# Follow-up work of the input projection in two queues instead of one, with scratch tiles of its own for gMLP

## The chip, the cores and the metric

One core of a Trainium2 chip runs one layer of a hybrid model in float32. The metric is the device time of the kernel in microseconds (us). The kernel before takes 3417.4 us, the median of 3 runs (3416.64 to 3420.89). The engines are named as in the profile: PE is TensorE (PEld its weight loads), DVE is VectorE, ACT is ScalarE, POOL is GpSimd, SP is SyncE.

## What is computed

640 tokens (512 latent ones on a grid, 128 of context) of width 2048 go through one layer:

- RMSNorm and modulation give h. `p = h @ w_in` has 5440 columns: r, k and v of 1024 columns each for 16 heads, low-rank inputs of 64, 64 and 160 columns, and u and v of 1024 each for 8 gMLP groups.
- The heads (RWKV-7): after a token shift, decays and gates are made from the low-rank inputs, and a delta-rule scan runs over the tokens in both directions:

```python
def step(S, inp):
    r_t, w_t, k_t, v_t, a_t, b_t = inp
    sa = jnp.einsum('bhvk,bhk->bhv', S, a_t)
    S = S * w_t[:, :, None, :] + sa[..., None] * b_t[:, :, None, :] + v_t[..., None] * k_t[:, :, None, :]
    return S, jnp.einsum('bhvk,bhk->bhv', S, r_t)
```

- The gMLP groups: v is normalised and mixed over chunks of 128 tokens by a 128 x 128 matrix of its group, and multiplies gelu(u).
- The two halves together go through w_out, are added to x, and a gated feed-forward net (FFN) follows.

## The kernel before

The profiled span falls into stages: the start (0 to 139 us: loads, RMSNorm, the first part of w_mod, the three low-rank blocks of w_in), the **w_in stage** (139 to 1163.5), its drain, the recurrence of the heads (until about 1495) with half of w_out between its steps, the other half of w_out (to 1662), and the FFN (to the end).

**The w_in stage.** w_in is worked on in 43 blocks of 128 columns. The order is the three low-rank ones, then for each pair of heads p = 0 to 7 its r, v and k block; one gMLP group (a v block, "gv", and a u block, "gu") stands behind each of pairs 0, 2, 4 and 5, and four groups behind pair 7 (`GORD`). A block has four pieces of 512 rows. `split` (L157 to 161) loads a piece, rounds its high half on ACT (L160) and makes the low half on DVE (L161), two pieces ahead. `win` then does 24 big matmuls per piece (L182 to 184: high by high, high by low, low by high half of h), into two PSUM tiles "big".

**Follow-up work.** When a block is done, `take` copies the PSUM to a tile "praw" and puts a generator on a queue, an object of class `Mixer`. A generator issues a few instructions and yields a number, its cost for the queue. `between`, called between the big matmuls, lets each queue run on by some cost per call: `max(AMIN, left / ADIV)` (1.5, 12.0) for the blocks' queue, where `left` is the sum of costs still queued.

- `take_r` and `take_v` shift r and v. `take_k` (queued with KCOST = 35, though its yields sum to about 52) makes, for both directions d, decays and gates (PE: pwa, L568; weights wh and wl, L532 and 533), the scaled tiles R, X, Z, the Gram matrices pG (L629, evicted to GB by ACT L635 and to GA by DVE L638), the transposes pXT (L645) and products pW (L654). It stores the results in DRAM (d_S) and the blocks of GB in "dd".
- `solve(p)` is put on the queue `mixS` at the end of take_k: it loads dd as "gi", and inverts 16 x 16 triangles by 15 steps of a multiply (L772) and a reduction (L774) on DVE, copies (ACT L778) and stores (POOL L781).
- `merge(p)` follows on `mixM`: it loads the triangles as TB (POOL L791) and for d = 0 and 1 joins them to 64 x 64 inverses by five groups of small matmuls (pblk L811 three times, pM L837, pT L846), evicts (TF, ACT L849) and stores to d_S (POOL L851). take_k's second half waits for the merge of an earlier pair before it makes a new GB.
- `take_gv` runs a gelu, transposes (pvt2, L703), and a normalisation to vt on DVE (to L727). `take_gu` runs a gelu and the mixing matmuls psp (L740) with vt, and stores to d_o.

**What sets the order.** All the blocks' follow-up generators stand in one first-in, first-out queue, `mixA`. Before a block's copy, `mixA.finish(b - RAW)` with RAW = 3 runs the queue until the work on block b - 3 has ended, since the praw tiles are three; what it issues then stands on PE without win matmuls between. Behind the last block all queues are drained in turn: mixA, mixS, mixM. The modulation of later stages (pm, L872, with 1 MB tiles of w_mod) is issued by piece.

The pools of this stage are closed at its end. The next ones use their space: the tiles "oh" and "ol" of w_out's inputs (big<-oh, L1002, is its first matmul), and x1T with its transposes pxT (L1260). The recurrence's small matmuls are w_ps (L1134), u_ps (L1149), y_ps (L1100 and 1105), s_ps (L1170) and swap (L1074).

Scratch: take_k's ssq and L, gelu2's gq and gv's gsq share the tag "t2" of the pool `bp`, tha and gu's sp the tag "t3", and v's vt and gv's vt2 the tag "vt" (one buffer).

Of the kernel before, what the change touches and what calls it, by code (L numbers as in the profile page):

```python
# [10 lines left out]
F32 = mybir.dt.float32  # L11
# [8 lines left out]
P = 128  # L20
D = 2048
KB = D // P
T = 640
NT = T // P
# [6 lines left out]
DA = 1024  # L31
NPAIR = DA // P
CSH = 3360
# [5 lines left out]
LEAD = 2  # L39
AMIN = 1.5  # L40
ADIV = 12.0
RAW = 3
SMIN = 3.0
GRAN = (1, 3)
SDIV = 9.0
# [40 lines left out]
def flow_step(ctx: ExitStack, tc, x_prompt, x_sample, state_rwkv, c, c_ctx, w_mod, b_mod,  # L86
# [3 lines left out]
    nc = tc.nc  # L90
# [112 lines left out]
    FIRST = (3072, 3200, 3328)  # L203
# [153 lines left out]
    bk, bp, gs, bz = (hp.enter_context(tc.tile_pool(name=n, bufs=1)) for n in ("bk", "bp", "gs", "bz"))  # L357
# [88 lines left out]
    def shifted(dst, pr, b, n=P):  # L446

        dst, pr = dst[:n, :], pr[:n, :]
        for (lo, hi, v) in SEG:
            S.activation(dst[:, lo:hi], pr[:, lo:hi], AF.Copy, scale=(c0c if v else c0l)[:n, b:b + 1])  # L450
        yield 0.4

        def add(e, o, i, m):
            e.scalar_tensor_tensor(out=o, in0=i, scalar=mucol(m, b)[:n, :], in1=o, op0=ALU.mult, op1=ALU.add)
        d3, q3 = v3(dst), v3(pr)
        add(V, d3[:, :, 1:CH], q3[:, :, 0:CH - 1], 0)
        yield 0.8
        add(V, d3[:, :, 0:CH - 1], q3[:, :, 1:CH], 1)
        yield 0.8
        add(V, dst[:, 320:321], pr[:, 319:320], 0)  # L460
        add(V, dst[:, 319:320], pr[:, 320:321], 1)
        for (o, i, n_) in ((64, 0, 192), (384, 192, 64), (448, 384, 192)):
            add(SH, dst[:, o:o + n_], pr[:, i:i + n_], 2)
            add(SH, dst[:, i:i + n_], pr[:, o:o + n_], 3)
        yield 0.6
# [31 lines left out]

    pairs = [Pair() for _ in range(NPAIR)]

    def take_r(pr, p):  # L500
        o = pairs[p]
        o.zr = bk.tile([P, T], F32, tag="zr", name="zr", bufs=2)
        yield from shifted(o.zr, pr, p)

    def take_v(pr, p):
        o = pairs[p]
        o.zv = bk.tile([P, T], F32, tag="zv", name="zv", bufs=1)
        yield from shifted(o.zv, pr, 16 + p)
        yield 1.5
        vt = bp.tile([P, NT, P], F32, tag="vt", name="vt", bufs=1)  # L510
        for (t0, t1) in ((0, 4), (4, 5)):
            ps = pt_.tile([P, 4, P], F32, tag="pt", name="pvt")
            for t in range(t0, t1):
                TE.transpose(ps[:, t - t0, :], o.zv[:, t * P:(t + 1) * P], ident)
            S.copy(vt[:, t0:t1, :], ps[:, 0:t1 - t0, :])
            yield 0.5
        nc.sync.dma_start(d_vt[p, 0].rearrange("(q t) v -> t q v", t=P), vt)
        nc.sync.dma_start(c3(d_vt[p, 1]), c3(d_vt[p, 0])[:, ::-1])

    def take_k(pr, p):  # L520
        o = pairs[p]
        o.GB, o.dd = {}, {}
        zr, zv = o.zr, o.zv
# [12 lines left out]

        yield from load_wl(0)
        yield from shifted(zk, pr, 8 + p)

        nkk = bk.tile([P, T], F32, tag="nkk", name="nkk", bufs=1)  # L540
        V.tensor_scalar_mul(nkk, zk, prm[:, C_KK + p:C_KK + p + 1])
        sq = bk.tile([P, T], F32, tag="t1", name="sqk", bufs=2)
# [14 lines left out]
        for d in range(2):  # L557
# [47 lines left out]
            f = fs if d == 0 else bk.tile([P, T], F32, tag="t1", name="f", bufs=2)  # L605
# [16 lines left out]
            n = 2 * p + d  # L622
# [50 lines left out]

    def gelu2(xx):

        sq = bp.tile([P, T], F32, tag="t2", name="gq")
        S.activation(sq, xx, AF.Square)
        yield 0.4
        V.tensor_scalar(sq, sq, GC1, 1.0, op0=ALU.mult, op1=ALU.add)
        V.tensor_mul(sq, sq, xx)  # L680
        yield 1.2
        S.activation(sq, sq, AF.Tanh, scale=GC0)
        yield 0.6
        V.scalar_tensor_tensor(out=xx, in0=sq, scalar=1.0, in1=xx, op0=ALU.add, op1=ALU.mult)
        yield 0.8

    vts = [None] * 8

    def take_gv(vv, g):
        lng, lnb, wsp = (gs.tile([P, P], F32, tag=n, name=n) for n in ("lng", "lnb", "wsp"))  # L690
        nc.sync.dma_start(lng, gmlp_ln_g[0, g].partition_broadcast(P))
        nc.sync.dma_start(lnb, gmlp_ln_b[0, g].partition_broadcast(P))
        nc.sync.dma_start(wsp, w_spatial[0, g])
        yield from gelu2(vv)
        pw = pt_.tile([P, 4, P], F32, tag="pt", name="pw")
        TE.transpose(pw[:, 0, :], wsp, ident)
        wspT = gs.tile([P, P], F32, name="wspT")
        S.copy(wspT, pw[:, 0, :])
        vt = bp.tile([P, NT, P], F32, tag="vt", name="vt2", bufs=1)
        for (t0, t1) in ((0, 4), (4, 5)):  # L700
            ps = pt_.tile([P, 4, P], F32, tag="pt", name="pvt2")
            for t in range(t0, t1):
                TE.transpose(ps[:, t - t0, :], vv[:, t * P:(t + 1) * P], ident)  # L703
            S.copy(vt[:, t0:t1, :], ps[:, 0:t1 - t0, :])
            yield 0.6
        bc = lambda ap: ap.unsqueeze(2).to_broadcast([P, NT, P])
        mn = gs.tile([P, NT], F32, name="gmn")
        V.tensor_reduce(out=mn, in_=vt, axis=AX.X, op=ALU.add)
        V.tensor_scalar_mul(mn, mn, 1.0 / P)
        yield 0.8  # L710
        V.tensor_tensor(out=vt, in0=vt, in1=bc(mn), op=ALU.subtract)
        yield 0.8
        sq = bp.tile([P, NT, P], F32, tag="t2", name="gsq")
        S.activation(sq, vt, AF.Square)
        yield 0.6
        va = gs.tile([P, NT], F32, name="gva")
        V.tensor_reduce(out=va, in_=sq, axis=AX.X, op=ALU.add)
        V.tensor_scalar(va, va, 1.0 / P, 4.0 * LN_EPS, op0=ALU.mult, op1=ALU.add)
        rstd = gs.tile([P, NT], F32, name="grs")
        rsqrt(rstd, va)  # L720
        yield 1.0
        yield 1.0
        V.tensor_tensor(out=vt, in0=vt, in1=bc(rstd), op=ALU.mult)
        yield 0.8
        fb = lambda ap: ap.unsqueeze(1).to_broadcast([P, NT, P])
        V.tensor_tensor(out=vt, in0=vt, in1=fb(lng), op=ALU.mult)
        V.tensor_tensor(out=vt, in0=vt, in1=fb(lnb), op=ALU.add)  # L727
        yield 1.5
        vts[g] = (vt, wspT)

    def take_gu(uu, g):
        bsp = gs.tile([P, P], F32, tag="wsp", name="bsp")
        nc.sync.dma_start(bsp, b_spatial[0, g].partition_broadcast(P))
        yield from gelu2(uu)
        vt, wspT = vts[g]
        sp = bp.tile([P, NT, P], F32, tag="t3", name="sp")
        for (t0, t1) in ((0, 4), (4, 5)):
            ps = pt_.tile([P, 4, P], F32, tag="pt", name="psp")
            for t in range(t0, t1):
                TE.matmul(ps[:, t - t0, :], vt[:, t, :], wspT, start=True, stop=True)  # L740
            V.tensor_tensor(out=sp[:, t0:t1, :], in0=ps[:, 0:t1 - t0, :],
                            in1=bsp.unsqueeze(1).to_broadcast([P, t1 - t0, P]), op=ALU.add)
            yield 0.6
        V.scalar_tensor_tensor(out=uu, in0=uu, scalar=0.5, in1=sp.rearrange("p t n -> p (t n)"),
                               op0=ALU.mult, op1=ALU.mult)
        yield 0.8
        nc.sync.dma_start(d_o[8 + g], uu)
        dump(f"o{8 + g}", uu)
# [140 lines left out]
            mod_cols(cur["tp"], ms, modc[g], tag=cur["tag"])  # L889
            yield  # L890

    blocks = [(FIRST[i], lambda h, i=i, n=n: low_rank(h, 24 + i, n), 3.2) for i, n in enumerate((P, P, 32))]

    def block(col, fn, cost, i):
        blocks.append((col, lambda pr: fn(pr, i), cost))

    g = 0
    for p in range(NPAIR):
        block(P * p, take_r, 2.6, p)
        block(2 * DA + P * p, take_v, 5.1, p)  # L900
        block(DA + P * p, take_k, KCOST, p)
        while g < GORD[p]:
            block(CSH + DA + P * g, take_gv, 12.0, g)
            block(CSH + P * g, take_gu, 5.0, g)
            g += 1
    pieces = [(b, q) for b in range(len(blocks)) for q in range(4)]
    parts = {}
# [3 lines left out]
            b, q = pieces[n]  # L911
            parts[n] = split(w_in[0, q * 512:(q + 1) * 512, blocks[b][0]:blocks[b][0] + P], 4)

    mixA, mixS, mixM = Mixer(), Mixer(), Mixer()
    cur.update(pool=bk, psum=pm_, tag="pt", raw="mraw")
    mods = mod_all()
    due = 0.0

    def take(b, halves):

        mixA.finish(b - RAW)
        pr = bp.tile([P, T], F32, tag="praw", name="praw", bufs=RAW)
        for hf in range(2):
            S.copy(pr[:, HALF * hf:HALF * hf + HALF], halves[hf])
        mixA.add(blocks[b][1](pr), blocks[b][2])

    def between(k):
        if k in GRAN:
            f = 1.0 / (2 * len(GRAN))
            mixA.run(f * max(AMIN, mixA.left / ADIV))  # L930
            mixS.run(f * SUBST)
            mixM.run(f * max(SMIN, mixM.left / SDIV), k == GRAN[-1])

# [10 lines left out]
    for n, (b, q) in list(enumerate(pieces))[N0:]:  # L944
# [7 lines left out]
        while due >= 1.0:  # L952
            due -= 1.0
            next(mods, None)
    mixA.drain()
    mixS.drain()
    mixM.drain()
    for _ in mods:
# [59 lines left out]
    with ExitStack() as ph:  # L1018
# [9 lines left out]
        gh, gl, gq = (rw.tile([P, T], F32R, name=n) for n in ("gh", "gl", "gq"))  # L1028
# [271 lines left out]
    t1, t2 = slice(0, HALF), slice(HALF, T)  # L1300
# [626 lines left out]
```

## Time and profile before

| what | value |
|---|---|
| median of 3 runs | 3417.4 us |
| the profiled execution, its own time | 3414.96 us |
| its span in the trace | 3413.2 us |
| granted TensorE clock, mean of the span | 0.975 |
| PE, DVE, ACT, POOL busy, share of the span | 93%, 74%, 43%, 37% |
| first and last w_in matmul behind the start | 139 us, 1163.5 us |
| first matmul of w_out | 1170.5 us |

Busy shares are of the whole span; a stage is read from the windows that the prediction shows. In a row of the waits, "PE pG L629 <- DVE X L618" says that pG's matmul at L629 stood on PE for a result of DVE's line 618. In a timeline row the first number is the start in us, the second the duration in us; "xN" counts records that run close together (PE's float32 matmul of the small kind leaves two records).

### The profile page before, as it was taken

What the parts mean: (1) busy time and instruction counts of PE and PEld (TensorE: products, weight loads), DVE (VectorE), ACT (ScalarE), POOL (GpSimd) and SP (SyncE); (2) the same over time, 40 slices, a digit from 0 to 9 for tenths busy, and PEclk for the clock granted to TensorE, in tenths of its full rate; (3) what the DMA queues carried; (4) which work ended last, traced back from release to release, by engine and by line L of the source; (5) the groups of instructions that cost most, each with busy time, mean ns of one, the idle gap of its engine ahead of it and who ended that gap; (6) DMA issues with size and microseconds to landing.
All of it is one profiled execution on the core that took longest, in us unless ns stands there. A gap on an engine that the chain in (4) does not pass through costs nothing.

```text
span 3413.2 us, 72346 instructions
## 1 busy us (share of the span) xinstructions
PE 3189.6 (93%) x28100; PEld 2905.1 (85%) x28100; DVE 2512.9 (74%) x4357; ACT 1451.5 (43%) x3172; POOL 1251.9 (37%) x1090
## 2 busy tenths in 40 slices
PE   6899989889988899989999999999999999999996
PEld 3688768768766877778999999999999999999986
DVE  4548577676766656656888888888878877877787
ACT  3334444444443433324644444444444444443365
POOL 0001121122112112321056565565666645555543
PEclk8999999999999899989999999999999999999998
DMA  8766676676767577735533434334343354543453
GB/s 322 242 191 200 194 195 175 168 204 180 198 185 193 149 221 238 219 112 158 171 113 115 125 105 126 120 110 124 112 123 113 116 178 141 153 148 114 146 165 115
DMA packets 719137, 552.94 MB, mean 162 GB/s; under 512 B 99449, under 2 KB 652425, under 8 KB 709961
## 3 DMA queue, kind: packets, MB, share of 16 engines
q1 hardware_dynamic: 706472, 534.61, 52.4%
q0 software_dynamic: 9984, 13.13, 2.0%
q8 instruction: 221, 3.62, 0.4%
q14 instruction: 124, 1.01, 0.1%
q10 hardware_dynamic: 2336, 0.57, 0.1%
HBM read 438.77 MB, written 111.69 MB: 161 GB/s over the span
## 4 chain that ended last, share of the span: by engine, by line
PE 50%; DVE 6%; issue 5%; DMA 3%; POOL 1%; ACT 1%; DVEq 0%; SPq 0%; ACTq 0%; POOLq 0%
PE P L1541 13%; PE P L1539 13%; PE P L1540 13%; DVE lo L1358 2%; PE big L1002 2%; DMA d_os<-act 1%; PE big L1003 1%; PE big L1004 1%; PE u_ps L1149 1%; PE y_ps L1105 1%; PE s_ps L1170 1%; PE pO L1217 1%; DVE act L1660 1%; PE big L1394 1%; PE big L1392 1%
## 5 line engine op out<-in xcount | busy, mean ns | idle before, releaser
L1541 PE MATMUL P<-xo,lo 128*128 128x320 f32 x2352 | 731.6, 311 | 11.1 <-DVE lo L1358 11.1
L1539 PE MATMUL P<-xo,hi 128*128 128x320 f32 x2352 | 728.2, 310 | 2.0 <-ACT hi L1357 2.0
L1540 PE MATMUL P<-xo,hi 128*128 128x320 f32 x2352 | 727.6, 309 | 0.0
L1358 DVE TENSOR_TENSOR lo<-raw,hi 128x512 fp32r<-128x512 f32 x532 | 585.9, 1120 | 64.1 <-ACT hi L1357 60.0
L1357 ACT CAST hi<-raw 128x512 fp32r<-128x512 f32 x532 | 326.4, 621 | 415.2 <-PE P L1540 320.4
L182 PE MATMUL big<-h_hi,hi 128*128 128x320 f32 x1376 | 452.1, 329 | 10.2 <-ACT h_hi L344 3.7
L1541 PEld LDWEIGHTS P<-xo,lo 128*128 128x128 f32 x2352 | 442.4, 188 | 18.9 <-DVE lo L1358 18.8
L1539 PEld LDWEIGHTS P<-xo,hi 128*128 128x128 f32 x2352 | 442.6, 188 | 2.9 <-ACT hi L1357 2.7
L1540 PEld LDWEIGHTS P<-xo,hi 128*128 128x128 f32 x2352 | 442.4, 188 | 0.0
L184 PE MATMUL big<-h_hi,lo 128*128 128x320 f32 x1376 | 436.6, 318 | 5.6 <-DVE lo L161 5.5
L183 PE MATMUL big<-h_lo,hi 128*128 128x320 f32 x1376 | 437.5, 318 | 0.5 <-DVE h_lo L345 0.5
L1452 POOL TENSOR_TENSOR raw<-raw 128x512 f32<-128x512 f32 x252 | 408.0, 1628 | 11.6 <-DVE lo L1358 1.6
L1541 PE MATMUL P<-xd,lo 128*128 128x320 f32 x1232 | 385.1, 313 | 17.8 <-DVE lo L1358 17.5
L1539 PE MATMUL P<-xd,hi 128*128 128x320 f32 x1232 | 383.7, 311 | 9.9 <-ACT hi L1357 6.8
L1540 PE MATMUL P<-xd,hi 128*128 128x320 f32 x1232 | 381.9, 310 | 0.0
L182 PEld LDWEIGHTS big<-h_hi,hi 128*128 128x128 f32 x1376 | 265.1, 193 | 76.8 <-issue 44.5
L161 DVE TENSOR_TENSOR lo<-raw,hi 128x512 fp32r<-128x512 f32 x268 | 185.7, 696 | 182.0 <-ACT hi L160 179.9
L160 ACT CAST hi<-raw 128x512 fp32r<-128x512 f32 x268 | 165.0, 618 | 295.1 <-PE big L183 122.2
L184 PEld LDWEIGHTS big<-h_hi,lo 128*128 128x128 f32 x1376 | 265.6, 193 | 12.7 <-DVE lo L161 7.4
L183 PEld LDWEIGHTS big<-h_lo,hi 128*128 128x128 f32 x1376 | 265.9, 193 | 7.9 <-issue 3.7
L1357 ACT CAST hi<-rawd 128x512 fp32r<-128x512 f32 (+1 forms) x288 | 168.7, 587 | 240.3 <-PE P L1540 222.6
L1452 POOL TENSOR_TENSOR t<-raw 128x512 f32<-128x512 f32 x84 | 135.8, 1617 | 343.1 <-DMA raw<-in_w_ffn_up_dram 325.7
(372 smaller groups left out, 6404.3 us busy)
## 6 DMA issues: line engine op xcount, KB each, us to landing
wt<-in_w_mod_dram SPq DMA_DIRECT2D x96, 1024.0 KB
raw<-in_w_ffn_gate_dram SPq DMA_DIRECT2D x182, 256.0 KB
raw<-in_w_ffn_up_dram SPq DMA_DIRECT2D x182, 256.0 KB
rec<-d_S SPq DMA_DIRECT2D x80, 576.0 KB
raw<-in_w_in_dram SPq DMA_DIRECT2D x172, 256.0 KB
rawd<-in_w_ffn_down_dram SPq DMA_DIRECT2D x128, 256.0 KB
raw<-in_w_out_dram SPq DMA_DIRECT2D x96, 256.0 KB
xd<-d_os SPq DMA_DIRECT2D x66, 320.0 KB
```

What stands on the lines that cost most here:

```text
L160: S.copy(hi, raw)
L161: V.tensor_sub(lo, raw, hi.bitcast(F32))
L182: TE.matmul(halves[hf], hi[:, k, :], h_hi[:, kb, s], start=(kb == 0), stop=False)
L183: TE.matmul(halves[hf], hi[:, k, :], h_lo[:, kb, s], start=False, stop=False)
L184: TE.matmul(halves[hf], lo[:, k, :], h_hi[:, kb, s], start=False, stop=(kb == KB - 1))
L1002: TE.matmul(halves[hf], hi[:, k, :], o_hi[kb][:, s], start=(k == 0), stop=False)
L1357: S.copy(hi[:, 0:nk], raw[:, 0:nk])
L1358: V.tensor_sub(lo[:, 0:nk], raw[:, 0:nk], hi[:, 0:nk].bitcast(F32))
L1452: G.tensor_tensor(out=o[:, 0:nk], in0=p[:, 0:nk], in1=q[:, 0:nk], op=ALU.subtract)
L1539: TE.matmul(ps, hi[:, k, :], xk[:, 0, :], start=f, stop=False)
L1540: TE.matmul(ps, hi[:, k, :], xk[:, 1, :], start=False, stop=False)
L1541: TE.matmul(ps, lo[:, k, :], xk[:, 0, :], start=False, stop=l)
```

## The change

- There are two queues for the blocks' follow-up work: mixA for pairs and low-rank blocks, mixB for gMLP blocks. `between` runs both, each by `max(AMIN, left / ADIV)` of its own.
- RAW is 4. `take(b)` no longer runs the queue until block b - 4 is done: it runs only the queue that owns block b - 4 until that block's praw tile has been read. take_r, take_v and take_k report this behind their shift (`read()`); the other blocks report it at their end.
- gMLP blocks get scratch tiles of their own: "u2" in place of "t2" and of "t3", "vt2" in place of "vt".
- Behind the last block mixA and mixB run in turn until both are empty, then mixS and mixM as before.
- The program is built with dynamic_dma_scratch_size=8192, a smaller ring for the descriptors of dynamic DMAs.

The number of instructions on each engine stays the same, and the last 14,056 rows of PE's order (the FFN and what stands just ahead of it) are the same too. Lines of the new kernel stand 3 higher from take_k to mod_all, and 15 higher from w_out on.

```diff
-RAW = 3
+RAW = 4
...
-    def take_k(pr, p):
+    def take_k(pr, p, read):
...
         yield from load_wl(0)
         yield from shifted(zk, pr, 8 + p)
+        read()
...
-        sq = bp.tile([P, T], F32, tag="t2", name="gq")
+        sq = bp.tile([P, T], F32, tag="u2", name="gq")
...
-        vt = bp.tile([P, NT, P], F32, tag="vt", name="vt2", bufs=1)
+        vt = bp.tile([P, NT, P], F32, tag="vt2", name="vt2", bufs=1)
...
-        sq = bp.tile([P, NT, P], F32, tag="t2", name="gsq")
+        sq = bp.tile([P, NT, P], F32, tag="u2", name="gsq")
...
-        sp = bp.tile([P, NT, P], F32, tag="t3", name="sp")
+        sp = bp.tile([P, NT, P], F32, tag="u2", name="sp")
...
+    mixA, mixB, mixS, mixM = Mixer(), Mixer(), Mixer(), Mixer()
+    free, owner = set(), {}
...
-            block(CSH + DA + P * g, take_gv, 12.0, g)
-            block(CSH + P * g, take_gu, 5.0, g)
+            block(CSH + DA + P * g, take_gv, 12.0, g, mixB)
+            block(CSH + P * g, take_gu, 5.0, g, mixB)
...
-        mixA.finish(b - RAW)
+        if b >= RAW:
+            owner[b - RAW].until(lambda: b - RAW in free)
         pr = bp.tile([P, T], F32, tag="praw", name="praw", bufs=RAW)
...
-        mixA.add(blocks[b][1](pr), blocks[b][2])
+        _, fn, cost, mix = blocks[b]
+
+        def task():
+            yield from fn(pr, lambda: free.add(b))
+            free.add(b)
+        owner[b] = mix
+        mix.add(task(), cost)
...
-            mixA.run(f * max(AMIN, mixA.left / ADIV))
+            for mix in (mixA, mixB):
+                mix.run(f * max(AMIN, mix.left / ADIV))
...
-    mixA.drain()
+    while mixA.q or mixB.q:
+        for mix in (mixA, mixB):
+            mix.hold, mix.budget = 0, 0.0
+            mix.run(1.0)
     mixS.drain()
     mixM.drain()
...
-    nc = _bacc.Bacc("TRN2", target_bir_lowering=False, num_devices=1)
+    nc = _bacc.Bacc("TRN2", target_bir_lowering=False, num_devices=1, dynamic_dma_scratch_size=8192)
```

What this does to the order of PE's instructions is seen at two places. The first is the end of w_in: the last win matmuls (L182 to 184), and what follows until the first w_out matmul (big<-oh, L1002). Before, one group of pair 7's merge (pM) and the last gMLP group's mixing (psp) stand there, with transposes of x1:

```order
L182 MATMUL big<-h_hi,hi 128x320
L183 MATMUL big<-h_lo,hi 128x320
L184 MATMUL big<-h_hi,lo 128x320
L837 MATMUL pM_13371<-TB,GB 32x32 x20
L740 MATMUL psp<-wspT,vt_13151 128x128 x4
L1260 MATMUL pxT<-ident,x1T 128x128 x2
L740 MATMUL psp<-wspT,vt_13151 128x128
L1260 MATMUL pxT<-ident,x1T 128x128 x2
L1002 MATMUL big<-oh,hi 128x320
```

After, the last win matmul is followed by pair 7's second direction (pwa, pG), with the last gMLP groups:

```order
L184 MATMUL big<-h_hi,lo 128x320
L571 MATMUL pwa<-waM,wh 128x320
L571 MATMUL pwa<-waM,wl 128x320
L571 MATMUL pwa<-waM,wh 128x320
L571 MATMUL pwa<-waM,wl 128x320
L699 MATMUL pw<-ident,wsp 128x128
L706 MATMUL pvt_12942<-ident,praw 128x128 x4
L706 MATMUL pvt_12948<-ident,praw 128x128
L632 MATMUL pG<-R,X 128x128 x8
L743 MATMUL psp<-wspT,vt_12941 128x128 x5
L632 MATMUL pG<-R,X 128x128 x12
```

35 rows further on stands the whole of pair 7's merge, with the recurrence's small matmuls ahead of it and behind it; w_out's first matmul (now L1017) comes 34 rows behind its last pT:

```order
L1164 MATMUL u_ps<-W,rec 64x64 x4
L814 MATMUL pblk<-TB,A__1127 32x32 x40
L814 MATMUL pblk<-M_13183,TB 32x32 x20
L814 MATMUL pblk<-TB,M_13183 32x32 x40
L840 MATMUL pM_13295<-TB,GB 32x32 x20
L849 MATMUL pT_13318<-TF,M_13294 32x32 x20
L814 MATMUL pblk<-TB,A__1127 32x32 x40
L814 MATMUL pblk<-M_13345,TB 32x32 x20
L814 MATMUL pblk<-TB,M_13345 32x32 x40
L840 MATMUL pM_13457<-TB,GB 32x32 x20
L849 MATMUL pT_13480<-TF,M_13456 32x32 x20
L1115 MATMUL y_ps<-ST,rec 64x64 x4
```

So all PE work that stood between the last win matmul and w_out before, some nine rows, has become some ninety, and pair 7's chain from pwa to merge is in it.

The second place is the second direction of a pair's K block inside the w_in stage. Before (pair 7), its three groups of pG stand close together among pieces of another pair's merge (pblk) and a gMLP block's transposes (pvt), with no win matmul in the rows shown:

```order
L629 MATMUL pG<-R,X 128x128 x8
L872 MATMUL pm_9805<-wt,cT 2x512 x4
L703 MATMUL pvt_11988<-ident,praw 128x128 x4
L811 MATMUL pblk<-TB,A__1127 32x32 x34
L629 MATMUL pG<-R,X 128x128 x8
L811 MATMUL pblk<-TB,A__1127 32x32 x6
L703 MATMUL pvt_12060<-ident,praw 128x128
L811 MATMUL pblk<-M_11976,TB 32x32 x20
L811 MATMUL pblk<-TB,M_11976 32x32 x17
L629 MATMUL pG<-R,X 128x128 x4
L811 MATMUL pblk<-TB,M_11976 32x32 x23
L837 MATMUL pM_12187<-TB,GB 32x32 x20
```

After (pair 6), win matmuls stand between them; the next group of pG comes 20 rows behind the first, the third 25 rows behind the second:

```order
L632 MATMUL pG<-R,X 128x128 x8
L875 MATMUL pm_9094<-wt,cT 2x512 x3
L182 MATMUL big<-h_hi,hi 128x320
L183 MATMUL big<-h_lo,hi 128x320
L184 MATMUL big<-h_hi,lo 128x320
L182 MATMUL big<-h_hi,hi 128x320
L183 MATMUL big<-h_lo,hi 128x320
L184 MATMUL big<-h_hi,lo 128x320
```

A step of the chain whose result is late thus has other PE work behind it in the queue, and ahead of the next step.

More of the change, by code (lines that the diff above doesn't have):

```diff
@@ L498, in flow_step, with take_r @@
     pairs = [Pair() for _ in range(NPAIR)]
-    def take_r(pr, p):
+    def take_r(pr, p, read):
         o = pairs[p]
@@ L503, in take_r, with take_v @@
         yield from shifted(o.zr, pr, p)
-    def take_v(pr, p):
+        read()
+    def take_v(pr, p, read):
         o = pairs[p]
@@ L508, in take_v @@
         yield from shifted(o.zv, pr, 16 + p)
+        read()
         yield 1.5
@@ L538, in take_k @@
         yield from shifted(zk, pr, 8 + p)
+        read()
         nkk = bk.tile([P, T], F32, tag="nkk", name="nkk", bufs=1)
@@ L687, in flow_step, with take_gv @@
     vts = [None] * 8
-    def take_gv(vv, g):
+    def take_gv(vv, g, read):
         lng, lnb, wsp = (gs.tile([P, P], F32, tag=n, name=n) for n in ("lng", "lnb", "wsp"))
@@ L729, in take_gv, with take_gu @@
         vts[g] = (vt, wspT)
-    def take_gu(uu, g):
+    def take_gu(uu, g, read):
         bsp = gs.tile([P, P], F32, tag="wsp", name="bsp")
@@ L890, in mod_all, with block @@
             yield
-    blocks = [(FIRST[i], lambda h, i=i, n=n: low_rank(h, 24 + i, n), 3.2) for i, n in enumerate((P, P, 32))]
-    def block(col, fn, cost, i):
-        blocks.append((col, lambda pr: fn(pr, i), cost))
+    mixA, mixB, mixS, mixM = Mixer(), Mixer(), Mixer(), Mixer()
+    free, owner = set(), {}
+    blocks = [(FIRST[i], lambda h, read, i=i, n=n: low_rank(h, 24 + i, n), 3.2, mixA) for i, n in enumerate((P, P, 32))]
+    def block(col, fn, cost, i, mix=mixA):
+        blocks.append((col, lambda pr, read: fn(pr, i, read), cost, mix))
     g = 0
@@ L912, in prefetch @@
             parts[n] = split(w_in[0, q * 512:(q + 1) * 512, blocks[b][0]:blocks[b][0] + P], 4)
-    mixA, mixS, mixM = Mixer(), Mixer(), Mixer()
     cur.update(pool=bk, psum=pm_, tag="pt", raw="mraw")
```

## The prediction

> **What bounds the kernel now.** I read first a table of windows, because the change touches one stage. The w_in stage runs from 139 us to the last w_in matmul at 1163.5; behind it come its drain, the recurrence beside w_out's first half, and later work whose instructions keep their order. Columns: window, length, busy time of each engine, then the granted TensorE clock (PEclk).
>
> ```profile
> 139.00:1163.50 1024.50, 936.30 (x10605) 787.91 (x10604) 701.53 (x1431) 443.77 (x950) 193.24 (x307) 0.97 0.68 185
> 1163.50:1192.00 28.50, 22.04 (x193) 20.12 (x194) 23.77 (x44) 13.30 (x27) 1.54 (x2) 0.82 0.63 201
> 1192.00:1495.00 303.00, 300.84 (x4412) 240.55 (x4405) 202.10 (x665) 106.40 (x486) 75.61 (x99) 1.00 0.72 214
> 151.00:215.00 64.00, 63.95 (x431) 58.08 (x431) 35.24 (x71) 23.23 (x43) 0.00 (x0) 1.00 0.56 169
> 716.00:750.00 34.00, 26.82 (x682) 20.85 (x683) 28.22 (x66) 18.20 (x43) 8.04 (x14) 1.00 0.76 208
> 1047.00:1103.00 56.00, 45.40 (x845) 35.74 (x846) 40.30 (x87) 25.06 (x58) 10.24 (x17) 0.93 0.66 179
> ```
>
> PE is the bound. In the w_in stage it idles 1024.5 - 936.3 = 88.2 us and runs at 0.97 of full clock. Without follow-up work waiting (151 to 215) it idles 0.05 us, so weights and their splitting keep up. In two stretches where take forces a block's follow-up work to its end (716 to 750, 1047 to 1103) it idles 7.2 and 10.6 us. From 1192 to 1495 it idles 2.2 of 303: whatever PE does not do before that stretch it must do in it, at its price. So I count PE's lost time from 139 to the first w_out matmul, not its work.
>
> The waits of PE in the w_in stage say what is late (total us, times, longest):
>
> ```profile
> PE pG L629 <- DVE X L618: 11.5, 10, 4.0
> PE pG L629 <- DVE GA L638: 10.8, 18, 1.9
> PE psp L740 <- DVE vt L727: 7.6, 3, 3.2
> PE pwa L568 <- DVE wl L533: 7.1, 2, 3.7
> PE pm L872 <- DMA wt<-in_w_mod_dram: 6.7, 8, 1.7
> PE pXT L645 <- DVE GA L638: 5.9, 6, 3.2
> PE big L184 <- DVE lo L161: 4.8, 3, 4.3
> PE psp L740 <- DVE mx L772: 3.0, 1, 3.0
> ```
>
> Nearly all are small matmuls of a follow-up chain whose DVE producer is not done when they reach the head of PE's queue; the one at L184 is a win matmul whose low half stands on DVE behind such a chain.
>
> **What the change removes from the w_in stage.** Before, take_gu's psp stands 39 to 61 rows behind its gv block's last transposes (pvt2) on PE; after, 256 to 362, except for the last blocks. I let the psp waits named above go but for those of the tail: 7.6 + 3.0 + some of the smaller ones, 13 in all. Before, a pair's K half stands in bunches, some with no win matmul between its three pG groups; after, each has win matmuls between its steps, and a half spreads over about 2.9 pieces of 24 big matmuls instead of 2.1. The distance from pwa to the first pG hardly grows (2.0 to 2.4 pieces), so of pG's 11.5 + 10.8 I take half, 11; of pwa's 7.1 six; of pXT's 5.9 three; of L184's 4.8 all, 5; of the other 88.2 - 57.4 = 30.8 in smaller rows a sixth, 5. The 6.7 on a load of w_mod stays. Sum 43 of 88. Bounds: 18, if only the psp waits and L184's go; 63, if only a tail like the quiet stretch's and the loads remain.
>
> The clock loses about 0.03 x 936 = 28 us there. If that follows the idle time, 28 x 43/88 = 14 come back (bounds 6 and 20). Pipeline bubbles between small groups: 4 (bounds 0 and 5). Saved in the stage: 43 + 14 + 4 = 61, bounds 24 and 88.
>
> **What it moves behind the last win matmul.** The pairs' queue now gets only its own share of steps, and gMLP blocks no longer force it on. By the order, pair 7's second half, its solve and its merge all stand behind the last win matmul, and the first w_out matmul behind that merge. The oh tiles take the SBUF of the pair queue's pools, so they wait for the last d_S<-TF store. Before, most of this was over:
>
> ```profile
> 1163.27 0.31 PE L184 MATMUL big<-h_hi,lo 128*128 128x320 f32 x1
> ...
> 1170.49 0.61 PE L1002 MATMUL big<-oh,hi 128*128 128x320 f32 x1
> ```
>
> Pair 7's own chain before gives the length of the new tail (timeline rows: start, duration; then the DVE lines of solve with total and mean ns; the medians from issue to landing; and a step of merge):
>
> ```profile
> 1054.87 0.53 ACT L571 ACTIVATE sg<-pwa,w0h 128x320 f32<-128x320 f32 x1 [0.65 <-PE pwa L568]
> ...
> 1075.69 0.54 ACT L635 COPY GB<-pG 64x128 f32<-64x128 f32 x2
> ...
> 1087.50 0.16 DVE L772 TENSOR_TENSOR mx<-mx,gi 80x2 f32<-80x2 f32 x1 [2.33 <-DMA gi<-dd]
> ...
> 1114.56 0.62 DVE L774 TENSOR_REDUCE mx<-mx 80x30 f32<-80x450 f32 x1
> ...
> 1121.29 5.32 POOL L791 DMA_DIRECT2D TB<-d  x8 [1.31 <-DMA d<-mx]
> ```
> ```profile
> L772 DVE TENSOR_TENSOR mx<-mx,gi 80x2 f32<-80x2 f32 (+14 forms) x120 | 53.5, 446 | 30.0 <-DMA gi<-dd 28.9
> L774 DVE TENSOR_REDUCE mx<-mx 80x2 f32<-80x2 f32 (+14 forms) x120 | 37.7, 314 | 1.1
> ```
> ```profile
> TB<-d POOLq DMA_DIRECT2D x64, 40.0 KB, 5.9
> d_S<-TF POOLq DMA_DIRECT2D x16, 320.0 KB, 5.6
> ```
> ```profile
> 724.52 0.89 PE L811 MATMUL pblk<-TB,A__1127 32*32 32x32 f32 x80
> ...
> 735.24 0.82 PE L846 MATMUL pT<-TF,M 32*32 32x32 f32 x40
> ...
> 755.74 0.85 ACT L849 COPY TF<-pT 32x320 f32<-32x320 f32 x2 [3.06 <-issue]
> ```
>
> Step by step: last win to the sigmoid's tanh, 1; from there to the last GB copy, 1054.87 to 1076.23, 21.4; to solve's first multiply, through dd and gi, 11.3; solve, 1087.50 to 1115.18, is 27.7 with DVE shared and (53.5 + 37.7)/8 = 11.4 alone: 20, the middle, since gv and gu still share DVE; from there to the end of issuing TB at 1126.61, 11.4; its landing about 5.2 more; merge, ten steps of matmuls and eviction: 10 x (0.82 + 0.85) = 17 by steps alone, 755.74 + 0.85 - 724.52 = 32 as pair 3's ran: 20, near the short end, since no win matmuls stand between its steps any more; the d_S store 5.6 and an oh cast, 7. Sum 97 (bounds 86 and 117).
>
> What can PE do meanwhile? The lines of its groups in the stage (total us before the bar's idle time) divide over 8 pairs or 16 halves:
>
> ```profile
> L629 PE MATMUL pG<-R,X 64*128 64x128 f32 x640 | 49.6, 290 | 22.6 <-DVE X L618 11.5 <-DVE GA L638 10.8
> L654 PE MATMUL pW<-Z,GA 64*64 64x64 f32 x640 | 25.9, 225 | 2.4 <-ACT XT L647 2.4
> L645 PE MATMUL pXT<-ident,X 128*128 128x128 f32 x160 | 25.3, 284 | 8.0 <-DVE GA L638 5.9 <-ACT XT L647 1.0 <-ACT A__1127 L797 0.8
> L740 PE MATMUL psp<-wspT,vt 128*128 128x128 f32 x80 | 14.5, 326 | 15.5 <-DVE vt L727 8.8 <-DVE mx L772 3.0 <-DVE TF L830 2.1
> L846 PE MATMUL pT<-TF,M 32*32 32x32 f32 x636 | 15.5, 193 | 0.8 <-issue 0.8
> ```
>
> The half: (49.6 + 25.9 + 25.3)/16 = 6.3, with pwa and pmm about 9. Merge: five groups like L846's, 5 x 15.5/8 = 10. The last gv and gu: 14.5/8 for psp, with transposes 3. The order also puts some 35 transposes of x1 and about 180 small matmuls of pair 0's first hops ahead of w_out:
>
> ```profile
> L1260 PE MATMUL pxT<-ident,x1T 128*128 128x128 f32 x55 | 10.6, 287 | 1.8 <-ACT x1T L1261 1.8
> ...
> 1309.02 0.69 PE L1170 MATMUL s_ps<-rec 128*64 128x64 f32 x16
> ```
>
> 35 x 10.6/55 = 7; a record is half of a matmul of the hops (the trace lists two for each), so 180 x 0.69/8 = 15. Half of the hops stand behind the merge and outlast d_S's landing by a little: 100 us until the first w_out matmul. That is 9 + 10 + 3 + 7 + 15 = 44 of 100, so PE idles 56 (bounds 45 and 76). At the clock of 1163.5 to 1192, 0.82, I add the same 4 that 22.04 us lose there (0.18 x 22.04). That window's loss before, 28.5 - 22.04 + 4 = 10.5, is replaced. Net cost of the tail: 56 + 4 - 10.5 = 50, bounds 38 and 70.
>
> A rule speaks against this: by the Trainium skill ("TensorE: Matmul & The Clock Gate", Part 1: The HAM clock gate), TensorE falls to half rate after about one idle window of 3.4 us. The rows agree in direction (0.82 where PE was idle a quarter of the time), yet 716 to 750 held 1.00 at 79% busy; what half rate would make of the sum is the second rival.
>
> For the landing of d_S the skill's fit ("DMA: Bandwidth & Descriptors", Anatomy of one DMA) gives about 2.75 us by an estimate from 320 KB, against the 5.6 measured; the tail would be 3 us shorter by it, and I keep the measured one.
>
> **Edits at nothing.** Reading the raw tile early and RAW=4 add one tile and no instruction. The smaller descriptor ring shows in no row; POOL is busy 193 of 1024 us in the stage, which hides a wait for ring entries, but in the tail TB's issues (5.32 us) lie on the path: 0, bounds -2 and +10. The shared u2 tile puts gMLP blocks behind one another, off the path until the last ones.
>
> **The sum.** -61 + 50 = -11; I take -10, since merge and solve have more room upwards. The profiled execution took 3414.96 (span 3413.2), 2.4 below the median of 3417.4; I take the difference from the median: 3407. About 0.2%, 7 us, is what a measurement of this kernel can tell from no change.
>
> **The rivals.**
>
> - The tail outweighs (slower). One mechanism: pair 7's serial chain behind the last win matmul. It decides from the point where PE's idle time in it exceeds what the w_in stage gives back. With solve and merge at their shared lengths (+8, +12) it costs 70; with 45 (pG's and pwa's waits staying, 16 less) from the stage: 3417 + 25 = 3442. For it: the windows on DVE that made solve long hold gv and gu work, which is in the tail too. Against: no win splits there. Chance 0.30.
> - The tail runs at half clock. The chain's own PE work, 9 + 10, then takes 19 longer, the rest hides in idle time; 4 of it are already counted: 3407 + 15 = 3422. That is the clock gate's rule above at its worst. No row shows less than 0.82. Chance 0.10.
> - The stage gets nearly dense and the tail is short. Solve alone (-9) and merge by steps (-3): tail 38; stage near its upper bound, 83: 3417 - 45 = 3372. For it: the quiet stretch's 0.05. Against: pG's distance hardly grows. Chance 0.16.
> - The change does little, or the ring costs. DVE's chains are as late as before and the tail is filled, or the small ring stalls POOL for 10: 3417 to 3427. Chance 0.08.
>
> The forecast itself has 0.36, its own range 3390 to 3420, so 0.28 of it is faster and 0.08 the same. Of the first rival 0.01 is the same, 0.29 slower; of the second 0.06 and 0.04; of the last 0.04 and 0.04. Faster 0.44, same 0.19, slower 0.37. The range runs from the third rival's 3372 to above the first's 3442, with its merge and solve at their upper bounds 3455; what is left out is the outer half of those two.
>
> **What would show it.** Right: from 139 to the last win matmul the stage is shorter by 60 to 90 us (some 20 of it work moved out), PE's idle there is near 45, psp's wait for vt is nearly gone; from the last win to the first w_out matmul 88 to 115 us, PE about 44% busy, and the recurrence ends later by less than the tail is longer. Wrong: PE idle in the stage still above 70; a first w_out matmul within 40 us; a FFN stage that changes by more than 5; or a tail above 125.

## The result, and the profile after

The changed kernel takes 3453.9 us, the median of 4 runs (3452.2 to 3455.6), beside 3419.1 us for the kernel before in the same comparison: a ratio of 1.0108, 95% interval 1.0094 to 1.0123. It is slower by some 35 us, where 3407 was forecast. The profiled executions are 38.1 us apart (spans 3451.3 and 3413.2).

The windows of the changed kernel, cut at the last win matmul (1124.1), the first w_out matmul (1238.1) and the start of w_out's other half (1533), in the columns of the prediction's first table:

```profile
139.00:1124.10 985.10, 920.56 (x10040) 781.66 (x10041) 679.33 (x1365) 428.80 (x917) 181.49 (x284) 0.96 0.67 184
1124.10:1238.10 114.00, 71.82 (x1064) 55.00 (x1062) 62.36 (x155) 35.14 (x101) 18.64 (x26) 0.52 0.60 171
1238.10:1533.00 294.90, 294.58 (x4102) 239.23 (x4103) 193.64 (x621) 100.69 (x447) 74.59 (x98) 0.99 0.67 201
```

The first matmul of w_out's other half comes at 1532.6 instead of 1495.1, 37.4 us later, and the spans end 38.1 apart, so nearly all the loss lies ahead of that point. (Behind it the distance wanders between 33 and 41 us; the FFN behind the last w_out matmul takes 1755.6 us instead of 1751.9.) From 139 us to the start of w_out's other half (cut at 1495 before, 1533 after) both kernels put the same instructions on PE:

| from 139 us to w_out's other half | elapsed | PE idle | PE busy |
|---|---|---|---|
| before | 1356.0 | 88.2 + 6.5 + 2.2 = 96.8 | 1259.2 |
| after | 1394.0 | 64.5 + 42.2 + 0.3 = 107.0 | 1287.0 |
| difference | +38.0 | +10.2 | +27.8 |

The idle time moved from one place to another and grew by 10. The larger part, 28 us, is the same PE work taking longer. The windows' clock says where most of it lies: 0.52 over the 114 us behind the last win matmul. One group shows how much longer. The 16 records of s_ps that the prediction shows at 0.69 us, at full clock, take twice that in the tail:

```profile
1169.02 1.44 PE L1185 MATMUL s_ps<-rec 128*64 128x64 f32 x16
```

The waits of PE in the w_in stage after (139 to 1124.1):

```profile
PE pm L875 <- DMA wt<-in_w_mod_dram: 7.5, 5, 2.8
PE pvt L516 <- DVE zv L454: 7.4, 5, 2.5
PE pG L632 <- DVE X L621: 7.1, 7, 1.7
PE pG L632 <- DVE GA L641: 5.6, 10, 1.0
PE pmm L491 <- DVE zv L672: 5.1, 2, 2.6
PE ptm L168 <- issue: 4.9, 1, 4.9
PE pmm L491 <- DVE mx L777: 4.7, 1, 4.7
```

psp's waits are gone, pG's fell from 22.3 to 12.7, and pwa's are gone; other small matmuls (pvt, pmm) now stand for DVE at the head of PE's queue. But the last pair's half has left this window, and its waits with it. Behind the last win matmul (1124.1 to 1238.1) stand:

```profile
PE pblk L814 <- ACT M L821: 8.3, 2, 7.7
PE pG L632 <- DVE X L621: 7.6, 1, 7.6
PE pG L632 <- DVE GA L641: 2.5, 1, 2.5
```

With these pG's waits are 22.8 us in all, as much as before. Behind the last win matmul (1123.85) pair 7's chain runs as the order said. These are rows of the timeline, of several engines:

```profile
1123.85 0.31 PE L184 MATMUL big<-h_hi,lo 128*128 128x320 f32 x1
1124.89 0.53 ACT L574 ACTIVATE sg<-pwa,w0h 128x320 f32<-128x320 f32 x1
...
1151.05 0.54 ACT L638 COPY GB<-pG 64x128 f32<-64x128 f32 x2 [2.94 <-PE pG L632]
...
1165.11 0.16 DVE L775 TENSOR_TENSOR mx<-mx,gi 80x2 f32<-80x2 f32 x1 [4.57 <-DMA gi<-dd]
...
1180.87 0.61 DVE L777 TENSOR_REDUCE mx<-mx 80x30 f32<-80x450 f32 x1
...
1188.58 5.27 POOL L794 DMA_DIRECT2D TB<-d  x8 [3.32 <-DMA d<-mx]
...
1203.67 0.72 ACT L1004 CAST oh<-ol 128x640 fp32r<-128x640 f32 x1 [4.10 <-DMA ol<-d_o]
1204.89 1.22 PE L814 MATMUL pblk<-M,TB 32*32 32x32 f32 x37 [7.69 <-ACT M L821]
...
1219.27 0.84 ACT L852 COPY TF<-pT 32x320 f32<-32x320 f32 x2 [2.11 <-issue]
...
1238.08 0.90 PE L1017 MATMUL big<-oh,hi 128*128 128x320 f32 x2
```

The last line is the first w_out matmul, 114 us behind the last win matmul (100 foretold, 7 before). Between 1220 and 1238 there is no wait to speak of: PE works on the recurrence's first hops, at half clock.

```profile
1221.00:1237.00 16.00, 15.43 (x172) 12.17 (x172) 3.50 (x14) 4.69 (x31) 0.62 (x1) 0.50 0.87 267
```

### The profile page after: what moved, and what is told of

It is laid out like the page before. It is cut to its first block, busy times and chain, and to the rows that moved or that the text cites. A ratio compares the mean times of both kernels' runs of the same rounds, so it can differ in the third digit from the quotient of the medians.

```text
span 3451.3 us, 72369 instructions
## 1 busy us (share of the span) xinstructions
PE 3211.3 (93%) x28100; PEld 2926.1 (85%) x28100; DVE 2506.5 (73%) x4357; ACT 1452.3 (42%) x3172; POOL 1257.3 (36%) x1090
## 4 chain that ended last, share of the span: by engine, by line
PE 48%; DVE 6%; issue 5%; DMA 4%; POOL 1%; ACT 1%; DVEq 0%; SPq 0%; ACTq 0%; POOLq 0%
PE P L1556 13%; PE P L1555 12%; PE P L1554 12%; DVE lo L1373 2%; DMA d_os<-act 2%; PE big L1017 2%; PE big L1018 1%; PE big L1019 1%; PE y_ps L1120 1%; DVE act L1675 1%; PE u_ps L1164 1%; PE pO L1232 1%; PE s_ps L1185 1%; PE y_ps L1115 1%; PE big L1407 0%
## 5 line engine op out<-in xcount | busy, mean ns | idle before, releaser
L1556 PE MATMUL P<-xo,lo 128*128 128x320 f32 x2352 | 732.2, 311 | 12.4 <-DVE lo L1373 12.4
L182 PE MATMUL big<-h_hi,hi 128*128 128x320 f32 x1376 | 455.7, 331 | 11.1 <-ACT hi L160 5.2
L184 PE MATMUL big<-h_hi,lo 128*128 128x320 f32 x1376 | 435.8, 318 | 1.7 <-DVE lo L161 1.7
L182 PEld LDWEIGHTS big<-h_hi,hi 128*128 128x128 f32 x1376 | 266.9, 194 | 78.4 <-issue 44.2
L184 PEld LDWEIGHTS big<-h_hi,lo 128*128 128x128 f32 x1376 | 265.2, 193 | 8.4 <-DVE lo L161 3.4
```

The source lines that it names most:

```text
L182: TE.matmul(halves[hf], hi[:, k, :], h_hi[:, kb, s], start=(kb == 0), stop=False)
L184: TE.matmul(halves[hf], lo[:, k, :], h_hi[:, kb, s], start=False, stop=(kb == KB - 1))
L1556: TE.matmul(ps, lo[:, k, :], xk[:, 0, :], start=False, stop=l)
```

## The experiments

Theory A: the pair queue's lateness alone, pair 7's chain behind the last win matmul, costs the time. Theory B: the smaller ring moves all left-hand tiles down by 8192 bytes while those of the right-hand pools stay; by my reckoning of the addresses, which no trace shows, the first oh and ol tiles lay on take_k's tiles before and lie on tiles of merge now, so w_out cannot start beside merge. Theory C: the half clock in the tail is the larger cost. Repeated executions in these comparisons spread by about 0.6%, so the intervals count, not single runs. Each run was profiled once, and the profiled execution lies up to 9 us off the median (3436.8 beside 3428.1 in the run with one queue), so small differences between two profiles say little.

**The ring alone.** The kernel before, with one line changed:

```diff
-    nc = _bacc.Bacc("TRN2", target_bir_lowering=False, num_devices=1)
+    nc = _bacc.Bacc("TRN2", target_bir_lowering=False, num_devices=1, dynamic_dma_scratch_size=8192)
```

> The kernel before with nothing changed but dynamic_dma_scratch_size=8192. Theory A (pair 7's late chain alone made the new kernel slow): the order of follow-up work in the w_in stage is that of before, so the time is within 5 us of before. Theory B (addresses): the smaller ring moves every tile of the left-hand pools down by 8192 bytes, the first oh and ol tiles now lie on TB and A1_ of merge and no longer on take_k's tiles, so the first w_out matmul waits for pair 7's merge: it comes 25 to 45 us later than 1170.5, the stretch before it holds few big matmuls at a clock near 0.5 to 0.7, and the time is 15 to 30 us above before.

Measured: 3436.0, ratio 1.0055 (1.0038 to 1.0071), 19 us over before's 3417.0. The windows of this run, up to the first w_out matmul and beyond:

```profile
139.00:1166.90 1027.90, 944.27 (x10607) 794.88 (x10605) 700.13 (x1428) 441.54 (x946) 193.68 (x307) 0.96 0.67 183
1166.90:1210.30 43.40, 29.14 (x318) 22.31 (x318) 27.37 (x60) 17.09 (x51) 3.11 (x3) 0.57 0.61 195
1210.30:1511.00 300.70, 300.17 (x4274) 242.62 (x4274) 201.77 (x650) 105.02 (x465) 74.58 (x98) 1.00 0.70 211
```

The first w_out matmul comes 44 us behind the last win matmul instead of 7, at a clock of 0.57 between. Theory B's effect is real, without a second queue. The timeline shows the wait: before, six loads of ol were issued by 1138.2, ahead of the last win matmul. Here two are, and the next four go out at 1205.86, just behind the landing (at 1205.7) of the last store of pair 7's merge:

```profile
1198.05 1.00 POOL L851 DMA_DIRECT2D d_S<-TF  x1 [9.28 <-ACT TF L849]
...
1205.86 1.76 SPq L988 DMA_DIRECT2D ol<-d_o  x4
...
1210.93 0.41 PE L1002 MATMUL big<-oh,hi 128*128 128x320 f32 x1
```

In the changed kernel, too, four loads of ol go out at 1225.17, behind the landing of that store at 1225.0. Idle time is 98.4 in all, only 1.6 more than before; PE busy is 1273.6, 14.4 more. The loss is again in PE's busy time, beside a stretch at a low clock.

**The ring, with the old addresses.** The same, with an unused tile of 8192 bytes opened first:

```diff
+    pad = cp.tile([P, 2048], F32, name="pad")
+    G.memset(pad[:, 0:1], 0.0)
     ident = cp.tile([P, P], F32, name="ident")
```

> The kernel before with the smaller ring, as in the first experiment, but with an unused tile of 8192 bytes per partition opened first, so that all tiles have the addresses they had before the change. If the 19 us of the smaller ring came from the addresses, the first w_out matmul is back within 8 us of the last win matmul and the time within 6 us of before. If the smaller ring itself makes dynamic DMAs wait, the time stays 10 to 25 us above before.

Measured: 3422.1, ratio 1.0025 (1.0008 to 1.0042), 6.5 over before's 3415.6. The first w_out matmul is back at 7 us behind the last win matmul (1172.3 to 1179.5), and six loads of ol are out by 1147.6. So about two thirds of the 19 us were the addresses. The rest, 3 to 14 us by the interval, goes with the ring. PE's order is that of before, yet PE idles 92.7 us in the stage instead of 88.2; psp's waits are 6 us longer than before here, but not in the run above, so no row names the cause and it stays open.

**One queue, the rest as changed.**

```diff
-    mixA, mixB, mixS, mixM = Mixer(), Mixer(), Mixer(), Mixer()
+    mixA, mixS, mixM = Mixer(), Mixer(), Mixer()
+    mixB = mixA
...
-            for mix in (mixA, mixB):
+            for mix in (mixA,):
...
```

> The changed kernel with all blocks in one queue again (mixB is mixA); RAW = 4, the early report of the read, the scratch tiles and the ring stay as changed. Theory A (the second queue makes the pairs late): pair 7's second direction now ends ahead of the last win matmul, so the stretch to the first w_out matmul is 20 to 35 us shorter than the 114 us of the changed kernel, while PE's idle time in the w_in stage rises from 64 towards 80: the sum is 10 to 25 us below the changed kernel. Theory B (addresses): w_out still stands behind all of merge 7 at half clock, so at most 15 us are gained.

Measured: 3428.1, ratio 1.0036 (1.0020 to 1.0053), 26 below the changed kernel. The stretch to w_out is 86 us, the forecast 20 to 35 less than 114:

```profile
139.00:1127.60 988.60, 917.22 (x10115) 775.60 (x10115) 693.29 (x1408) 432.80 (x932) 184.31 (x295) 0.98 0.68 188
1127.60:1213.50 85.90, 58.47 (x945) 45.69 (x945) 47.14 (x106) 28.71 (x85) 10.67 (x15) 0.54 0.57 162
```

PE idles 71.4 in the stage, 7 more than with two queues and 12 less than with the ring alone (1027.9 - 944.27 = 83.6). So by these profiles most of the stage's gain is RAW = 4, the early report and the scratch tiles; the second queue takes another 7 out there, little more than the 4.5 by which two profiles of one order differed above, and makes the tail 28 us longer. By the medians against before: ring +19, the other parts in one queue -8 beside it (the intervals overlap, so this one is not clear of noise), the second queue +26.

**The pools in another order.** The changed kernel, so that oh and ol lie on take_k's tiles again:

```diff
-    bk, bp, gs, bz = (hp.enter_context(tc.tile_pool(name=n, bufs=1)) for n in ("bk", "bp", "gs", "bz"))
+    gs, bk, bv, bp, bz = (hp.enter_context(tc.tile_pool(name=n, bufs=1)) for n in ("gs", "bk", "bv", "bp", "bz"))
...
-        vt = bp.tile([P, NT, P], F32, tag="vt", name="vt", bufs=1)
+        vt = bv.tile([P, NT, P], F32, tag="vt", name="vt", bufs=1)
```

> The changed kernel with the same queues and the same costs, but the pools opened in another order (gs, bk, take_v's vt in a pool of its own, bp, bz), so that the first oh and ol tiles lie on take_k's tiles again and not on TB and A1_. Theory A (the length of pair 7's chain sets the end): at most 10 us less than the changed kernel, since the chain is as late. Theory B (addresses): the first w_out matmul comes behind pair 7's second direction and not behind its merge, 45 to 65 us after the last win matmul instead of 114; solve and merge run beside w_out, the half clock ends there, and the time falls by 35 to 55 us, to 3400 to 3420.

Measured: 3443.3, ratio 1.0070 (1.0042 to 1.0098).

```profile
1128.90:1199.40 70.50, 39.21 (x310) 27.95 (x311) 48.01 (x120) 23.98 (x56) 15.61 (x21) 0.59 0.71 195
1199.40:1520.70 321.30, 317.12 (x4849) 257.06 (x4848) 206.39 (x653) 110.99 (x491) 78.20 (x103) 0.98 0.68 201
```

w_out starts 43 us sooner, though 70.5 us are more than the 45 to 65 of theory B, and only some 10 us are gained, at the edge of what the intervals tell apart: theory B's size is wrong here. The work left out of the tail is done behind its end instead (294.9 us became 321.3), and pair 7's second direction alone still leaves 31 us idle and 39 at 0.59. Addresses matter, but most of the changed kernel's tail is the late pair.

**Faster queues.** The changed kernel with `KCOST = 52.0` and `ADIV = 6.0`:

> The changed kernel with KCOST = 52 (what take_k's yields add up to) and ADIV = 6, so both queues run faster and pair 7's K block and half of its merge stand ahead of the last win matmul. Theory A: the stretch to the first w_out matmul shrinks from 114 to 40 to 55 us and the time falls by 35 to 50 us, to 3405 to 3420. Theory B: the same stretch, but what is left of it is still without w_out's matmuls and at half clock; the time falls by 20 to 35. Both: PE's idle time in the w_in stage grows by 5 to 15, since steps stand closer together.

Measured: 3400.3, ratio 0.9949 (0.9922 to 0.9976): 54 below the changed kernel, 17 below before. The tail is 22 us:

```profile
139.00:1150.70 1011.70, 930.70 (x10503) 786.70 (x10501) 720.19 (x1444) 445.17 (x954) 196.81 (x306) 0.97 0.67 187
1150.70:1172.80 22.10, 15.76 (x271) 11.47 (x271) 11.02 (x21) 11.05 (x23) 2.05 (x4) 0.65 0.76 229
1172.80:1483.50 310.70, 310.19 (x4425) 250.25 (x4423) 206.67 (x671) 107.11 (x485) 74.57 (x98) 0.99 0.70 211
```

The price is 81.0 idle in the stage instead of 64.5, a little more than the 5 to 15 expected. The time is below theory A's range, and the tail shorter than its 40 to 55.

**More work in the tail.** The changed kernel with big matmuls on h that nobody reads:

```diff
+    dm = pb.tile([P, HALF], F32, tag="big", name="warm")
+
+    def warm(n):
+        for _ in range(n):
+            TE.matmul(dm, h_hi[:, 0, 0:P], h_hi[:, 0, 0:HALF], start=True, stop=True)
...
             mix.hold, mix.budget = 0, 0.0
             mix.run(1.0)
+        warm(4)
-    mixS.drain()
-    mixM.drain()
+    for mix, n in ((mixS, 4), (mixM, 3)):
+        while mix.q:
+            mix.hold, mix.budget = 0, 0.0
+            mix.run(0.01)
+            warm(n)
```

> The changed kernel with 206 additional big matmuls on h, whose result nobody reads, placed in the stretch behind the last win matmul, ahead of pair 7's merge. They are 206 x 0.148 = 30 us of PE at full clock. Theory C (the tail's cost is mostly the half clock): PE's clock stays near 1.0 from the last win matmul to the end of pair 7's solve, its real matmuls there take their full-clock times, and the added 30 us lie in idle time; the time falls by 5 to 20 us although work was added. Theory A (the cost is the chain's length on DVE, POOL and DMA): the clock rises as well, but the time stays within 4 us or rises by up to 15, since PE waits for other engines anyway.

Measured: 3451.7, ratio 1.0101 (1.0074 to 1.0127), as without them. Two windows, in the tail's first part with the added work, and among the hops without it:

```profile
1125.00:1160.00 35.00, 32.20 (x260) 29.02 (x259) 24.65 (x46) 11.90 (x28) 9.19 (x11) 1.00 0.45 116
1222.00:1236.00 14.00, 13.93 (x162) 10.86 (x158) 4.47 (x18) 5.41 (x33) 0.00 (x0) 0.50 0.96 293
```

The clock does come back while the added matmuls run. From the last win matmul to w_out's other half PE idles 22.8 us instead of 42.5 and is busy 387.5 instead of 366.4, 21 more though 30 were added: the clock gave back some 9, idle time took up 20, and the added work used both. Theory A's time held (within 4 us of the changed kernel) and theory C's fall of 5 to 20 did not come. As a balance it says that half clock in that first part costs about 9 us. Behind it, merge and hops still ran at 0.50.

**Was it the second queue?** The kernel before with `KCOST = 52.0` and `ADIV = 6.0`:

> The kernel before (one queue, RAW = 3, shared scratch, old ring) with KCOST = 52 and ADIV = 6 alone. If the two queues with their scratch tiles take anything out of the w_in stage, this stays 10 to 20 us above the two-queue kernel with the same two numbers (3400), at 3408 to 3420, with 85 to 95 us of PE idle in the stage. If the two numbers alone did it, it comes to 3395 to 3405.

Measured: 3402.7, ratio 0.9944 (0.9924 to 0.9963), the same as two queues with these numbers: the two numbers alone did it. Then with `KCOST = 52.0` alone:

> The kernel before with KCOST = 52 alone (ADIV = 12). If the old queue was only slow because it counted take_k at 35, forced bunches get rarer and the time lies between before and the kernel with both numbers: 3402 to 3412. If the shorter time constant did it, it stays within 5 us of before.

Measured: 3389.7, ratio 0.9928 (0.9902 to 0.9954), the lowest median of all and below the expected range, though its interval overlaps those of the runs with both numbers. Why it is below them was not looked into. Its w_in stage has 76 us of idle and no tail:

```profile
139.00:1147.40 1008.40, 932.39 (x10610) 783.85 (x10610) 714.27 (x1444) 447.08 (x954) 195.43 (x307) 0.98 0.68 188
1147.40:1472.00 324.60, 319.27 (x4567) 257.32 (x4567) 217.05 (x692) 117.02 (x505) 78.26 (x101) 0.99 0.71 215
```

**Two queues at their best.** With the pool order of above and `KCOST = 52.0`, `ADIV = 6.0`:

> Two queues with KCOST = 52 and ADIV = 6, and the pools in the order that keeps the first oh and ol tiles off TB and A1_. Theory B (addresses matter as long as merge 7 ends behind the last win matmul): the first w_out matmul comes within 8 us of the last win matmul instead of 22, so 5 to 12 us less than the same kernel without the pool order (3400): 3388 to 3396. Theory A (pair 7 on time is all that counts): within 4 us of 3400.

Measured: 3403.0, ratio 0.9962 (0.9947 to 0.9977), no better than without the pool order, as theory A said, though w_out now starts 3 us behind the last win matmul. With `ADIV = 8.0`:

> Two queues with KCOST = 52, ADIV = 8 and the pool order: the pairs' steps are spread wider than with 6, and pair 7's whole merge stands behind the last win matmul, though w_out is free to run beside it. Theory B: PE idle in the w_in stage is some 5 us less than with 6, and the late merge costs little because big matmuls surround it: 3384 to 3396, equal to the kernel with 6 or a little better. Theory A: the late merge costs its chain again, 10 us or more above the kernel with 6.

Measured: 3415.8, ratio 0.9992 (0.9977 to 1.0006): 20 over the range of theory B, and 13 above the kernel with 6, as theory A had it. With `GORD = (1, 1, 1, 2, 2, 3, 3, 8)` as well, to see whether the late merge did that:

> Two queues, KCOST = 52, ADIV = 8, the pool order, and GORD = (1, 1, 1, 2, 2, 3, 3, 8), which puts five gMLP groups behind pair 7 and not four. Pair 7's merge ends ahead of the last win matmul, so the drain holds only the last gMLP group, as before. If pair 7's lateness made the kernel with ADIV = 8 and the pool order slow (3416), this falls to 3392 to 3404. If the spread steps in the w_in stage are what costs, it stays within 5 us of 3416.

Measured: 3416.6, ratio 0.9999 (0.9985 to 1.0013). Pair 7's merge is done ahead of the last win matmul here, and it made no difference, so the late merge was not the reason. In both, PE idles 90 to 97 us in the stage; the waits of pG in the first of the two:

```profile
PE pG L632 <- DVE GA L641: 18.4, 16, 4.0
PE pG L632 <- DVE X L621: 17.1, 10, 3.7
PE big L184 <- DVE lo L161: 10.8, 5, 6.3
```

They are the waits that the second queue was to remove. The changed kernel had 12.7 of pG's in the stage; with `KCOST = 52.0` and `ADIV = 6.0` the same two rows are 31.1 already, so it is not the 8 that brings them back. What does was not settled.

## Why the prediction was wrong, point by point

The first rival named the outcome: the tail outweighs. It did so by a longer solve and merge, which did not come: solve took 16.4 us, not the shared 27.7, and merge with the landing of TB 26.3 where the forecast had 25. The forecast's sum was -11, the profiles are 38 apart. In idle time it had -43 + 56 - 6.5 = +6.5 and +10.2 was measured; in clock and bubbles it had -18 (the tail's 4 and the drain's 4 cancel) and PE's busy time grew by 27.8. By its own steps:

- **"Sum 43 of 88"**: 23.7 idle us went (88.2 to 64.5). The psp and L184 waits went as forecast, pwa's too and pG's fell by 9.6 of the 11, but others took some 20 us in their place (pvt on zv 7.4, pmm on zv and mx 9.8, ptm 4.9), and pG's came back in the tail. A chain whose DVE step is late shows at whichever PE step comes next; I let waits go row by row as if nothing stood behind them.
- **"14 come back" of the clock**: nothing did. The stage's clock was 0.96, not above the 0.97 of before. Idle time fell but the clock did not follow it. The 4 for bubbles between small groups came from no row, and no run here shows it.
- **"Sum 97", "100 us until the first w_out matmul"**: 114. pwa to GB 26.7 (21.4), GB to solve 13.5 (11.3), solve 16.4 (20), to the end of TB's issue 12.4 (11.4), then 26.3 to the last TF copy (25 with the landing), where 7.7 went on a copy queued on ACT behind oh's cast, which waited for its load. The hops behind the merge took 18, against 10 foretold (7 for d_S's store and a cast, 3 beyond it); they kept PE busy at half clock, so here the clock lengthened the path itself.
- **"PE idles 56"**: 42.2. The balance of idle time came out nearly right by luck: the stage gave back 19 less than forecast, and the tail cost 14 less.
- **"At the clock of 1163.5 to 1192, 0.82, I add the same 4"**: this is the step that failed. It carried the clock of a drain that idled 6.5 of 28.5 us over to a tail that idles 42.2 of 114 and holds no big matmuls. The clock there was 0.52, so what the forecast counted as 44 us of work took 71.8. Clock was to give 14 back; PE's busy time grew by 27.8. The second rival named it, priced at 15 with a chance of 0.10, as an alternative to a long tail; both came at once.
- **The ring, "0, bounds -2 and +10"**: +19, two thirds of it by addresses. The text said that the oh tiles take the SBUF of the pair queue's pools, but took this as a property of both kernels; with the old addresses w_out does not wait for merge.

None of the four signs of being wrong that the prediction named appeared: idle in the stage 64.5, the first w_out matmul 114 us behind the last win matmul (neither within 40 nor above 125), the FFN 3.7 longer. None of them looked at the clock. A sign of being right did tell: PE was busy 63% of the tail and not 44%.

The Trainium skill's rule weighed there ("TensorE: Matmul & The Clock Gate", Part 1: The HAM clock gate) gives half rate behind an idle window, and full rate again after about 3.4 us of sustained work. The trace agrees with the first part (0.52 in the tail, with 42.2 of 114 us idle). It does not agree with the second for the hops: 1221 to 1237 is 15.43 of 16 us busy at 0.50.

## What to carry to other kernels

When a queue's budget per step follows what it still holds, two queues in place of one make each step smaller: see which of them still holds work behind the last step that could cover it. Here one cost put right (52 for 35) gained 26 us, and the second queue lost as much. A buffer size is also an address: see which tiles a later pool lands on before and after. Cost work that is moved out of a dense stretch at the clock of a sparse one, and look at busy time, not only at idle time, when two traces are compared.

## What the runs showed of the hardware

Small matmuls did not bring the clock back. The hops' float32 matmuls (64 x 64 and 128 x 64) kept PE busy for 15.43 of 16 us at a granted clock of 0.50, and 13.93 of 14 in the run with added matmuls; there 128 x 320 matmuls in the gaps of the tail's first part held 1.00 at 32.20 of 35. In the changed kernel the clock came back with w_out's 128 x 320 matmuls: 0.50 from 1238.1 to 1243.5, 1.00 from 1243.7 to 1250. That the size of the matmuls is the reason was not tested by itself.
